# Second block's grouped attention: TensorE in the program's order, with half a gate tile between the parts of each step

## The chip, the cores and the metric

The kernel runs on one core of one Trainium2 chip. The metric is the time of one execution in microseconds (us), as the device measures it, and versions are compared by the median of several executions. The core's engines are named as in the profile: PE is TensorE's matmul side and PEld its weight loads, DVE is VectorE, ACT is ScalarE, POOL is GpSimd, and SP is SyncE, which here issues the loads from HBM.

## What is computed

The kernel computes two transformer blocks over 512 positions of width 1024. The change lies in the second block, between its recurrent branch (an mLSTM, `ym`) and the merge of two branches. Cut to what matters:

```python
scores = einsum(q, k)                    # 8 query heads on 2 key/value heads, 128-wide blocks
scores = where(valid, scores + bias, NEG_INF)
probs  = softmax(concat([scores, sink]))[..., :-1]
ya     = einsum(probs, v)                # grouped windowed attention
gates  = sigmoid(mg + merge_b)           # mg = h @ (merge columns of w_in), 2048 wide
u = gates[..., :1024] * (ya @ w_branch_attn) + gates[..., 1024:] * (ym @ w_branch_mlstm)
x = x + u @ w_out                        # then a mixture of 32 experts
```

The merge gates `mg` need only the normed input `h`. They depend neither on the attention `ya` nor on the recurrent branch `ym`.

## The kernel before

A scheduler at build time orders each engine's instructions by the program's order as a priority and by its own estimate of when their inputs are ready, so that work written later can stand between work written earlier. Inside `tc.manual_schedule(engines={PE})` it leaves PE's instructions in the order in which the program writes them, and still orders DVE, ACT and the others itself.

A dense product in this kernel is a tile of 128 outputs by 512 positions. `parts` splits the 512 KB of weights `wr` into a high part `wh` (ACT, L260) and a low part `wl` (DVE, L261), and `mm3` issues three matmuls for each of 8 slices of 128 inputs (L277 to L279), so a tile is 24 matmuls. The input is `hh` and `hl`, which the trace names `bh` and `bl` after their buffer; the sum lands in one of two PSUM buffers `d`. Small products use six PSUM buffers `m`.

At the place of the change the program writes, in this order:

- the end of the mLSTM. Per block of 128 positions POOL makes a norm (`rstd`), DVE applies it (L1247), and PE transposes the four heads (L1251). Then DVE (L1253, `nt`) and ACT and DVE (L260, L261, the trace's `hl<-nt`) make the split result `ym`, head by head.
- the attention, `_gqa`. Five groups of four transposes (L1290) bring queries and keys into place, ACT copies each group to `qk` (L1291). Then come 16 steps (t, i): four pairs of heads t, and four blocks of queries i. `scores(t, i)` multiplies queries and keys for the pair (PE, L1306, 256 keys wide at the first and last block and 384 in between), DVE adds the bias and takes the maximum (L1312), ACT exponentiates (L1317), DVE normalizes (L1318 to L1321) into `S`. `values(t, i)` transposes `S` (PE, L1333) and ACT copies it to `PT` (L1334); at i = 3 PE multiplies the whole pair's `PT` with the values (L1341) and the sum is split into `yah` and `yal`. `_pipelined` writes `scores` of a step and then `values` of the step before it.
- gate tiles 0 to 7: `mtanh(m)` computes a tile of `mg` and ACT takes its tanh (L700) into `tha`, which stays until the merge.
- the merge, `_merge`, which for each m computes gate tile 8 + m and then the two branch products.

Before the change nothing fixes PE's order here, and the scheduler puts matmuls of gate tiles 0 to 4 in the gaps of the mLSTM's end and of the attention.

Of the kernel before, what the change touches and what calls it, by code (L numbers as in the profile page):

```python
# [13 lines left out]
AF = mybir.ActivationFunctionType  # L14
# [3 lines left out]
P = 128  # L18
# [164 lines left out]
def _prog(ctx, tc, nc, I, out):  # L183
    PE, DVE, ACT, POOL, SP = nc.tensor, nc.vector, nc.scalar, nc.gpsimd, nc.sync
# [15 lines left out]
    def pt(pool, shape, tag, dt=F32, bufs=None):  # L200
        kw = {} if bufs is None else {"bufs": bufs}
        return pool.tile(shape, dt, tag=tag, name=nm(tag), **kw)
# [8 lines left out]
    def psd():  # L211
        return pt(pd, [P, 512], "d")
# [40 lines left out]
    def col(name, j=0, n=1):  # L253
        o, _ = _COLS[name]
        if kept:
            return kept[0][:, o - _COLS["final_norm_w"][0] + j :][:, :n]
        return cols[:, o + j : o + j + n]
# [5 lines left out]
    def raw(src, n=1024):  # L263
        r = ptx(W, [P, 1024], "wr")
        SP.dma_start(r[:, :n], src)
        return r[:, :n]

    def parts(r, pool=W):

        n = int(r.shape[1])  # L270
        hi, lo = (ptx(W, [P, 1024], n, F32R) if pool is W else pt(pool, [P, 1024], n, F32R, bufs=4) for n in ("wh", "wl"))
        split(hi[:, :n], lo[:, :n], r)
        return hi, lo

    def mm3(ps, w, x, first, last):
        (wh, wl), (xh, xl) = w, x
        PE.matmul(ps, lhsT=wh, rhs=xh, start=first, stop=False)  # L277
        PE.matmul(ps, lhsT=wl, rhs=xh, start=False, stop=False)  # L278
        PE.matmul(ps, lhsT=wh, rhs=xl, start=False, stop=last)  # L279

    def tile_a(src, x, kt=8, m=P):

        w = parts(raw(src, kt * m))
        ps = psd()
        for k in range(kt):
            mm3(ps[:m], [t[:, k * m : (k + 1) * m] for t in w], [t[:, k, :] for t in x], k == 0, k == kt - 1)
        ada_step()
        return ps
# [163 lines left out]
    def ada_step():  # L452
        if late[0]:
            late[0] -= 1
            late[1] += 1
            return
        next(ada_steps, None)
        if late[1]:
            late[1] -= 1
            next(ada_steps, None)  # L460
# [6 lines left out]
    with xps:  # L467

        hh = pt(HB, [P, 8, 512], "hh", F32R)
        hl = pt(HB, [P, 8, 512], "hl", F32R)  # L470
# [125 lines left out]
        hh = pt(HB, [P, 8, 512], "bh", F32R)  # L596
        hl = pt(HB, [P, 8, 512], "bl", F32R)
# [28 lines left out]
        with tc.tile_pool(name="ffn", bufs=2, reuse_waits="tile") as FF:  # L626
            x = (hh, hl)
            for part, (a, b) in enumerate(_PARTS):
                ah = pt(HB, [P, 8, 512], "hh", F32R)
                al = pt(HB, [P, 8, 512], "hl", F32R)  # L630
                for m in range(a, b):
                    y = []
                    for j in range(2):
                        ps = ups.pop(0) if ups else tile_a(I["w_up"][2 * m + j], x)
# [12 lines left out]
                for m in range(8 if part < 2 else 5):  # L647
                    ps = tile_a(dn(m), (ah, al), kt=b - a)
# [5 lines left out]
            hh = pt(HB, [P, 8, 512], "bh", F32R)  # L654
            hl = pt(HB, [P, 8, 512], "bl", F32R)
# [28 lines left out]
    with tc.tile_pool(name="b2", bufs=1, reuse_waits="tile") as B2:  # L684

        ym = pt(HB, [P, 8, 512], "hl", F32R)
        ymh, yml = ym[:, :4], ym[:, 4:]
        qkv = pt(B2, [P, 4, 768], "qkv")
        with tc.tile_pool(name="mq", bufs=1, reuse_waits="tile") as MQ:
            _mlstm(locals(), MQ)  # L690
        with tc.tile_pool(name="b2y", bufs=1, reuse_waits="tile") as B3:
            ya = pt(HB, [P, 8, 512], "hh", F32R)
            yah, yal = ya[:, :4], ya[:, 4:]
            mb = pt(B3, [P, 16], "mb")
            DVE.tensor_scalar(mb, col("merge_b", 0, 16), 0.5, None, op0=ALU.mult)

            def mtanh(m, pool):

                t = pt(pool, [P, 512], "tha%d" % m if m < 8 else "th", bufs=1 if m < 8 else 2)
                ACT.activation(t, tile_a(I["w2_mg"][m], (hh, hl)), AF.Tanh, bias=mb[:, m : m + 1], scale=0.5)  # L700
                return t

            _gqa(locals())
            tha = [mtanh(m, B3) for m in range(8)]
            xws.close()
            for n in places.values():
                n[1] = 0
            us = ExitStack()
            U = us.enter_context(tc.tile_pool(name="u", bufs=1, side="right", reuse_waits="tile"))
            uh = pt(U, [P, 8, 512], "uh", F32R)  # L710
            ul = pt(U, [P, 8, 512], "ul", F32R)
            _merge(locals())
# [558 lines left out]
def _gqa(env):  # L1271
    tc, nc, I, PE, DVE, ACT, POOL, SP = _names(env, "tc nc I PE DVE ACT POOL SP")
    pt, psd, psm, col, split = _names(env, "pt psd psm col split")
    yah, yal, qkv, sm, ident, pers = _names(env, "yah yal qkv sm ident pers")
    XW = env["XW"]
    rstd = env["rstd"]
    with tc.tile_pool(name="ga", bufs=1, reuse_waits="tile") as M:

        def bias_tile(h):
            b = pt(M, [P, 384], "bias", bufs=4)  # L1280
            SP.dma_start(b, I["t5b"][h])
            return b

        gq = pt(M, [P, 1], "gq")
        DVE.tensor_scalar(gq, col("q_gain"), 0.125, None, op0=ALU.mult)
        qk = pt(M, [P, 5, 512], "qk")
        for m in (4, 0, 1, 2, 3):
            ps = psm()
            for t in range(4):
                PE.transpose(ps[:, t * P : (t + 1) * P], qkv[:, t, m * P : (m + 1) * P], ident)  # L1290
            ACT.activation(qk[:, m, :], ps, AF.Copy, scale=gq if m < 4 else col("k_gain"))  # L1291
        state = {}

        def scores(t, i):
            if i == 0:
                state[t] = ([pt(M, [P, 10, P], "PT", bufs=3) for _ in range(2)], [bias_tile(2 * t), bias_tile(2 * t + 1)])
            _, bias = state[t]
            sink = col("sink", 2 * t, 2)
            J = range(max(0, i - 1), min(4, i + 2))
            n = len(J) * P  # L1300
            b0 = P if i == 0 else 0
            pss, Ss = [], []
            for e in range(2):
                ps = psm()
                r = slice(64 * e, 64 * e + 64)
                PE.matmul(ps[:, :n], lhsT=qk[r, t, i * P : (i + 1) * P], rhs=qk[r, 4, J[0] * P : J[0] * P + n], start=True, stop=True)  # L1306
                pss.append(ps)
            st = pt(sm, [P, 10], "st2", bufs=8)
            for e in range(2):
                S = pt(M, [P, 384], "S", bufs=6)  # L1310
                Ss.append(S)
                DVE.tensor_tensor_reduce(out=S[:, :n], in0=pss[e][:, :n], in1=bias[e][:, b0 : b0 + n], scale=1.0, scalar=sink[:, e : e + 1], op0=ALU.add, op1=ALU.max, accum_out=st[:, e : e + 1])  # L1312
            DVE.tensor_scalar(st[:, 2:4], st[:, 0:2], -1.0, None, op0=ALU.mult)
            DVE.tensor_tensor(st[:, 4:6], sink, st[:, 0:2], op=ALU.subtract)
            ACT.activation(st[:, 4:6], st[:, 4:6], AF.Exp)
            for e in range(2):
                ACT.activation(Ss[e][:, :n], Ss[e][:, :n], AF.Exp, bias=st[:, 2 + e : 3 + e], accum_out=st[:, 6 + e : 7 + e])  # L1317
            DVE.tensor_tensor(st[:, 4:6], st[:, 4:6], st[:, 6:8], op=ALU.add)  # L1318
            DVE.reciprocal(st[:, 8:10], st[:, 4:6])
            for e in range(2):  # L1320
                DVE.tensor_scalar(Ss[e][:, :n], Ss[e][:, :n], st[:, 8 + e : 9 + e], None, op0=ALU.mult)  # L1321
            return Ss

        bases = (0, 2, 5, 8)

        def values(t, i, Ss):
            PT, _ = state[t]
            J = range(max(0, i - 1), min(4, i + 2))
            n = len(J)
            for e in range(2):  # L1330
                tp = psm()
                for j in range(n):
                    PE.transpose(tp[:, j * P : (j + 1) * P], Ss[e][:, j * P : (j + 1) * P], ident)  # L1333
                ACT.activation(PT[e][:, bases[i] : bases[i] + n, :], tp[:, : n * P].rearrange("p (j q) -> p j q", j=n), AF.Copy)  # L1334
            if i == 3:
                po = psm()
                for i in range(4):
                    J = range(max(0, i - 1), min(4, i + 2))
                    for x, j in enumerate(J):
                        for e in range(2):  # L1340
                            PE.matmul(po[64 * e : 64 * e + 64, i * P : (i + 1) * P], lhsT=qkv[:, j, 640 + 64 * e : 704 + 64 * e], rhs=PT[e][:, bases[i] + x, :], start=(x == 0), stop=(x == len(J) - 1))  # L1341
                split(yah[:, t, :], yal[:, t, :], po)

        _pipelined([(t, i) for t in range(4) for i in range(4)], scores, values)


# [365 lines left out]
```

## Time and profile before

| what | value |
|---|---|
| three runs | 1588.38, 1591.37, 1591.61 us; median 1591.37 us |
| the profiled execution | 1588.89 us, of which 1587.1 us is the span between the first and the last instruction |
| busy PE, DVE, ACT in the span | 1550.4, 850.4, 524.4 us |
| granted TensorE clock, mean over the span | 0.992 of full speed |

The span is the stretch that the trace covers; what lies around it is 1.8 us. Times in the rows are counted from its start. Matmul records overlap, since one begins before the record of the one ahead has ended, so the pace of a run of matmuls is read from their starts and not from their durations.

### The profile page before, as it was taken

How to read it: one execution, taken by the hardware profiler on the slowest of the kernel's cores; microseconds unless marked ns; L12 is line 12 of the kernel's file. 1: busy time of each engine (PE TensorE's matmuls, PEld its weight loads, DVE VectorE, ACT ScalarE, POOL GpSimd, SP SyncE). 2: the span in 40 equal slices, each digit the busy share in tenths (PEclk: the TensorE clock that was granted, in tenths of full speed). 3: DMA queues.
4: the chain of work that ended last, by engine and by line, in shares of the span. 5: the costliest groups of instructions: out<-in, count | busy, mean ns of one | idle time of the engine just before them, and what ended most of it. 6: DMA issues, size and time to landing. Idle time of an engine off the chain costs nothing.

```text
span 1587.1 us, 21111 instructions
## 1 busy us (share of the span) xinstructions
PE 1550.4 (98%) x8208; PEld 1106.1 (70%) x8208; DVE 850.4 (54%) x1679; ACT 524.4 (33%) x964; POOL 35.8 (2%) x33
## 2 busy tenths in 40 slices
PE   8999999999999999989999999999999999999997
PEld 7878857988888888978976688866535545545443
DVE  7777886674564466668467724454242332332333
ACT  4453375442442344443456722231101101101101
POOL 0002000000000000000101000000000000000000
PEclk8999999999999999999999999999999999999999
DMA  8365423333233234402201023497999999999992
GB/s 331 135 197 175 167 73 101 126 100 106 100 94 104 95 93 128 145 18 98 89 27 57 29 86 98 141 316 271 392 369 418 418 415 418 419 417 417 418 417 75
DMA packets 92598, 321.02 MB, mean 202 GB/s; under 512 B 10412, under 2 KB 13100, under 8 KB 91472
## 3 DMA queue, kind: packets, MB, share of 16 engines
q1 hardware_dynamic: 92496, 319.64, 54.1%
q8 instruction: 66, 1.08, 0.3%
q14 instruction: 36, 0.29, 0.1%
HBM read 315.41 MB, written 4.19 MB: 201 GB/s over the span
## 4 chain that ended last, share of the span: by engine, by line
PE 90%; DVE 5%; ACT 2%; DMA 1%; issue 1%; POOL 1%; SPq 0%; DVEq 0%; ACTq 0%
PE d L1522 21%; PE d L277 15%; PE d L278 15%; PE d L279 15%; PE m L1508 4%; PE m L1624 4%; PE m L277 1%; PE m L279 1%; PE m L278 1%; PE m L1219 1%; PE m L1204 1%; DMA wr<-w_ada 1%; PE m L1039 1%; POOL rstd L371 1%; ACT S L1317 1%
## 5 line engine op out<-in xcount | busy, mean ns | idle before, releaser
L1522 PE MATMUL d<-we,xg 128*64 128x512 f32 x1024 | 226.6, 595 | 0.0
L261 DVE TENSOR_TENSOR wl<-wr,wh 128x1024 fp32r<-128x1024 f32 (+1 forms) x148 | 178.1, 1206 | 79.7 <-ACT wh L260 79.1
L277 PE MATMUL d<-bh,wh 128*128 128x512 f32 (+1 forms) x544 | 210.3, 387 | 2.6 <-ACT bh L475 1.5
L279 PE MATMUL d<-bl,wh 128*128 128x512 f32 (+1 forms) x544 | 209.7, 385 | 0.0
L278 PE MATMUL d<-bh,wl 128*128 128x512 f32 (+1 forms) x544 | 209.6, 385 | 0.0
L260 ACT ACTIVATE wh<-wr 128x1024 fp32r<-128x1024 f32 (+1 forms) x148 | 154.0, 1044 | 147.5 <-PE d L279 120.2
L1522 PEld LDWEIGHTS d<-we,xg 128*64 128x64 f32 x1024 | 70.8, 137 | 134.4 <-issue 121.6
L277 PE MATMUL d<-hh,wh 128*128 128x512 f32 (+1 forms) x392 | 147.2, 376 | 0.7 <-ACT bh L845 0.7
L278 PE MATMUL d<-hh,wl 128*128 128x512 f32 (+1 forms) x392 | 145.9, 373 | 0.0
L279 PE MATMUL d<-hl,wh 128*128 128x512 f32 (+1 forms) x392 | 145.8, 373 | 0.0
L277 PEld LDWEIGHTS d<-bh,wh 128*128 128x128 f32 x544 | 102.4, 188 | 25.0 <-issue 2.2
L278 PEld LDWEIGHTS d<-bh,wl 128*128 128x128 f32 x544 | 102.4, 188 | 22.2 <-issue 2.6
L279 PEld LDWEIGHTS d<-bl,wh 128*128 128x128 f32 x544 | 102.6, 189 | 20.1 <-issue 0.5
L1522 PE MATMUL d<-we,aT 128*64 128x512 f32 x512 | 112.6, 592 | 0.7 <-ACT aT L1597 0.7
L1522 PEld LDWEIGHTS d<-we,aT 128*64 128x64 f32 x512 | 36.7, 137 | 73.5 <-issue 71.4
L1625 DVE TENSOR_TENSOR xt<-xt,m 128x512 f32<-128x512 f32 x120 | 73.8, 681 | 22.8 <-PE m L1624 22.8
L277 PEld LDWEIGHTS d<-hh,wh 128*128 128x128 f32 x392 | 73.8, 188 | 16.8 <-issue 2.3
L1608 ACT ACTIVATE yh<-d,ws 128x512 fp32r<-128x512 f32 x32 | 22.0, 688 | 185.2 <-PE d L1522 185.2
L279 PEld LDWEIGHTS d<-hl,wh 128*128 128x128 f32 x392 | 73.7, 188 | 13.7 <-issue 0.5
L278 PEld LDWEIGHTS d<-hh,wl 128*128 128x128 f32 x392 | 73.9, 188 | 12.5
L638 DVE SCALAR_TENSOR_TENSOR cv<-d,cols,cv 128x511 f32<-128x511 f32 x41 | 30.7, 749 | 77.3 <-ACT cv L637 77.3
L1597 ACT ACTIVATE aT<-m 128x512 f32<-128x512 f32 x16 | 9.6, 598 | 176.5 <-PE m L1595 176.5
(430 smaller groups left out, 2631.6 us busy)
## 6 DMA issues: line engine op xcount, KB each, us to landing
we<-w_eg SPq DMA_DIRECT2D x128, 512.0 KB, 9.9
we<-w_eu SPq DMA_DIRECT2D x128, 512.0 KB, 8.9
we<-w_ed SPq DMA_DIRECT2D x128, 512.0 KB, 9.9
wr<-w_up SPq DMA_DIRECT2D x44, 512.0 KB, 3.3
wr<-w_ada SPq DMA_DIRECT2D x32, 512.0 KB, 4.0
wr<-w_out SPq DMA_DIRECT2D x16, 512.0 KB, 3.5
wr<-w_dn SPq DMA_DIRECT2D x16, 512.0 KB, 3.6
wr<-w_mg SPq DMA_DIRECT2D x16, 512.0 KB, 3.3
```

Source lines behind the costliest of these rows:

```text
L260: ACT.activation(hi, src, AF.Copy)
L261: DVE.tensor_tensor(lo, src, hi.bitcast(F32), op=ALU.subtract)
L277: PE.matmul(ps, lhsT=wh, rhs=xh, start=first, stop=False)
L278: PE.matmul(ps, lhsT=wl, rhs=xh, start=False, stop=False)
L279: PE.matmul(ps, lhsT=wh, rhs=xl, start=False, stop=last)
L371: POOL.tensor_tensor(r, ms, mhalf.to_broadcast((P, n)), op=ALU.pow)
L638: DVE.scalar_tensor_tensor(o[:, 1:], ps[:, :511], wc(1), o[:, 1:], op0=ALU.mult, op1=ALU.add)
L1508: PE.matmul(ps[:, :n], lhsT=hx[:, T, d * P : (d + 1) * P], rhs=oh[:, T, :n], start=(T == 0 and hx is hth), stop=(T == 3 and hx is htl))
L1522: PE.matmul(ps[x * m : (x + 1) * m], lhsT=xs[x][:, k, :], rhs=w[k // 2][x][:, k % 2 * 512 : k % 2 * 512 + 512], start=(k == 0), stop=(k == ...
L1608: ACT.activation(yh[:, s], ps, AF.Copy, scale=ws)
L1624: PE.matmul(ps, lhsT=oht[:, T * P : (T + 1) * P], rhs=y[:, s], start=(i == 0), stop=(i == len(mm) - 1))
L1625: DVE.tensor_tensor(xt[:, T, s], xt[:, T, s] if len(done) > 1 else hth[:, T, s].bitcast(F32), ps, op=ALU.add)
```

## The change

`mtanh` can now take a finished PSUM tile. A generator `mtanhs` computes gate tiles 0 to 7 and gives control back after four and after eight of the eight slices of each tile, so it has 16 pieces of 12 matmuls. `scores` takes the next piece at its end, and PE is in the program's order inside `_gqa`. The tiles are no longer written behind the attention.

```diff
-            def mtanh(m, pool):
+            def mtanh(m, pool, ps=None):
 
                 t = pt(pool, [P, 512], "tha%d" % m if m < 8 else "th", bufs=1 if m < 8 else 2)
-                ACT.activation(t, tile_a(I["w2_mg"][m], (hh, hl)), AF.Tanh, bias=mb[:, m : m + 1], scale=0.5)
+                ACT.activation(t, tile_a(I["w2_mg"][m], (hh, hl)) if ps is None else ps, AF.Tanh, bias=mb[:, m : m + 1], scale=0.5)
                 return t
 
+            tha = []
+
+            def mtanhs():
+
+                for m in range(8):
+                    w = parts(raw(I["w2_mg"][m]))
+                    ps = psd()
+                    for k in range(8):
+                        mm3(ps, [t[:, k * P : (k + 1) * P] for t in w], (hh[:, k, :], hl[:, k, :]), k == 0, k == 7)
+                        if k == 3:
+                            yield
+                    tha.append(mtanh(m, B3, ps))
+                    yield
+
+            fill = mtanhs()
             _gqa(locals())
-            tha = [mtanh(m, B3) for m in range(8)]
...
-    with tc.tile_pool(name="ga", bufs=1, reuse_waits="tile") as M:
+    fill = env["fill"]
+    with tc.tile_pool(name="ga", bufs=1, reuse_waits="tile") as M, tc.manual_schedule(engines={mybir.EngineType.PE}):
...
                 DVE.tensor_scalar(Ss[e][:, :n], Ss[e][:, :n], st[:, 8 + e : 9 + e], None, op0=ALU.mult)
+            next(fill)
             return Ss
```

The number of PE, DVE, ACT and DMA instructions stays the same. Three places show what moved. Lines of the changed file are 14 to 16 higher than those of the old one.

First, PE at the seam between the mLSTM's end and the first scores. In the old order gate tile 0 (`d_7901`) stands between the last transposes of the mLSTM (L1251) and those of queries and keys (L1290):

```order
L277 MATMUL d_7901<-bh_5206,wh_7897 128x512
L1251 MATMUL m_7264<-k_ident_92,hh_6665 128x128
L1251 MATMUL m_7273<-k_ident_92,hh_6665 128x128
L1251 MATMUL m_7282<-k_ident_92,hh_6665 128x128
L1251 MATMUL m_7291<-k_ident_92,hh_6665 128x128
L278 MATMUL d_7901<-bh_5206,wl_7898 128x512
L279 MATMUL d_7901<-bl_5207,wh_7897 128x512
L277 MATMUL d_7901<-bh_5206,wh_7897 128x512
L1290 MATMUL m_7327<-k_ident_92,qkv_5783 128x128 x4
L278 MATMUL d_7901<-bh_5206,wl_7898 128x512
L1290 MATMUL m_7333<-k_ident_92,qkv_5783 128x128 x4
```

In the new order the same transposes (L1265, L1305) follow one another, and gate tile 0 (`d_7377`) begins behind the first scores (L1321):

```order
L1265 MATMUL m_7264<-k_ident_92,hh_6665 128x128
L1265 MATMUL m_7273<-k_ident_92,hh_6665 128x128
L1265 MATMUL m_7282<-k_ident_92,hh_6665 128x128
L1265 MATMUL m_7291<-k_ident_92,hh_6665 128x128
L1305 MATMUL m_7329<-k_ident_92,qkv_5783 128x128 x4
L1305 MATMUL m_7335<-k_ident_92,qkv_5783 128x128 x4
L1305 MATMUL m_7341<-k_ident_92,qkv_5783 128x128 x4
L1321 MATMUL m_7353<-qk_7316 128x256
L1321 MATMUL m_7355<-qk_7316 128x256
L277 MATMUL d_7377<-bh_5206,wh_7373 128x512
```

All 39 gate matmuls that the old order has ahead of its first scores (24 of tile 0 and 15 of tile 1) moved behind them.

Second, PE in the attention's loop. In the old order the transposes of `S` (L1333) and the scores (L1306) of two steps stand together, and pieces of gate tiles of 7 to 11 matmuls stand at eight places, 73 matmuls in all, before the last product with the values:

```order
L279 MATMUL d_7934<-bl_5207,wh_7930 128x512
L277 MATMUL d_7934<-bh_5206,wh_7930 128x512
L1333 MATMUL m_7387<-k_ident_92,S_7356 128x128 x2
L1333 MATMUL m_7391<-k_ident_92,S_7358 128x128 x2
L1306 MATMUL m_7395<-qk_7314 128x384
L1306 MATMUL m_7397<-qk_7314 128x384
L1333 MATMUL m_7413<-k_ident_92,S_7374 128x128 x3
L1333 MATMUL m_7418<-k_ident_92,S_7376 128x128 x3
L1306 MATMUL m_7423<-qk_7314 128x256
L1306 MATMUL m_7425<-qk_7314 128x256
L278 MATMUL d_7934<-bh_5206,wl_7931 128x512
```

In the new order each step's transposes (L1349) and the next scores (L1321) are followed by 12 gate matmuls, 16 times:

```order
L278 MATMUL d_7454<-bh_5206,wl_7451 128x512
L279 MATMUL d_7454<-bl_5207,wh_7450 128x512
L1349 MATMUL m_7467<-k_ident_92,S_7395 128x128 x3
L1349 MATMUL m_7472<-k_ident_92,S_7397 128x128 x3
L1321 MATMUL m_7477<-qk_7316 128x256
L1321 MATMUL m_7479<-qk_7316 128x256
L277 MATMUL d_7454<-bh_5206,wh_7450 128x512
L278 MATMUL d_7454<-bh_5206,wl_7451 128x512
```

All 192 matmuls of gate tiles 0 to 7 now stand inside the loop, and none behind it.

Third, ACT at the same seam. In the old order gate tile 0's tanh (L700) and the high part of a later gate tile's weights (`wh_7996`) stand ahead of the last head's split and of the copies to `qk` (L1291):

```order
L260 ACTIVATE hl_5782<-nt_7287 128x512
L700 ACTIVATE tha_7894<-d_7901,mb_7307 128x512
L260 ACTIVATE wh_7996<-wr_7994 128x1024
L260 ACTIVATE hl_5782<-nt_7296 128x512
L1291 ACTIVATE qk_7314<-m_7315,cols_76 128x512
L1291 ACTIVATE qk_7314<-m_7321,gq_7312 128x512
```

In the new order these two are not there:

```order
L260 ACTIVATE hl_5782<-nt_7287 128x512
L260 ACTIVATE hl_5782<-nt_7296 128x512
L1306 ACTIVATE qk_7316<-m_7317,cols_76 128x512
L1306 ACTIVATE qk_7316<-m_7323,gq_7314 128x512
L1306 ACTIVATE qk_7316<-m_7329,gq_7314 128x512
```

They moved into the loop, where tanh and split now alternate with the steps. On DVE the matching low part (`wl_7997`) moved likewise. In SP's queue the eight gate loads stay ahead of the bias loads, and the load for gate tile 8 now stands ahead of the last bias pair, no longer behind all of them. POOL's order is unchanged.

## Rows read from the trace of the kernel before

**Rows 1.** The page, part 1: busy us, share of span, instructions.

```profile
PE 1550.4 (98%) x8208; PEld 1106.1 (70%) x8208; DVE 850.4 (54%) x1679; ACT 524.4 (33%) x964; POOL 35.8 (2%) x33
```

**Rows 2.** Stretches: length, busy (instructions) of PE, PEld, DVE, ACT, POOL, clock, DMA.

```profile
843.30:860.18 16.88, 14.11 (x76) 10.48 (x75) 12.78 (x23) 7.38 (x12) 4.91 (x4) 1.00 0.23 78
860.18:914.64 54.46, 51.63 (x379) 35.39 (x378) 40.38 (x166) 39.42 (x124) 0.00 (x0) 1.00 0.11 35
932.70:1079.00 146.30, 145.91 (x639) 113.71 (x637) 67.44 (x84) 43.38 (x55) 0.00 (x0) 1.00 0.52 178
1092.00:1566.00 474.00, 473.01 (x2402) 227.27 (x2403) 157.22 (x327) 57.70 (x95) 0.00 (x0) 1.00 0.96 388
```

**Rows 3.** PE's timeline around the first scores: start, duration, instruction, [idle before, releaser].

```profile
843.32 0.39 PE L277 MATMUL d<-bh,wh 128*128 128x512 f32 x1
...
845.97 0.63 PE L1251 MATMUL m<-k_ident,hh 128*128 128x128 f32 x4 [0.90 <-DVE hh L1247]
...
852.73 0.66 PE L1251 MATMUL m<-k_ident,hh 128*128 128x128 f32 x4 [1.01 <-DVE hh L1247]
...
859.86 0.39 PE L279 MATMUL d<-bl,wh 128*128 128x512 f32 x1
860.18 1.35 PE L1306 MATMUL m<-qk 64*128 64x256 f32 x8
...
864.18 0.63 PE L1333 MATMUL m<-k_ident,S 128*128 128x128 f32 x4 [0.85 <-DVE S L1321]
```

**Rows 4.** Timeline of ACT and DVE ahead of the first scores.

```profile
856.67 0.67 ACT L700 ACTIVATE tha<-d,mb 128x512 f32<-128x512 f32 x1
856.80 0.75 DVE L1253 SCALAR_TENSOR_TENSOR nt<-m,gh,hh 128x512 f32<-128x512 f32 x1
...
857.24 1.05 ACT L260 ACTIVATE wh<-wr 128x1024 fp32r<-128x1024 f32 x1
...
858.19 0.62 ACT L260 ACTIVATE hl<-nt 128x512 fp32r<-128x512 f32 x1
...
858.32 1.23 DVE L261 TENSOR_TENSOR wl<-wr,wh 128x1024 fp32r<-128x1024 f32 x1
...
859.28 1.26 ACT L1291 ACTIVATE qk<-m,gq 128x512 f32<-128x512 f32 x2
```

**Rows 5.** ACT's timeline: tanh behind two gate tiles that follow one another.

```profile
922.23 0.69 ACT L700 ACTIVATE tha<-d,mb 128x512 f32<-128x512 f32 x1 [3.80 <-PE d L279]
927.67 0.69 ACT L700 ACTIVATE tha<-d,mb 128x512 f32<-128x512 f32 x1 [4.75 <-PE d L279]
```

**Rows 6.** PE's timeline in the attention's loop.

```profile
881.64 0.88 PE L1333 MATMUL m<-k_ident,S 128*128 128x128 f32 x6
882.45 0.70 PE L1306 MATMUL m<-qk 64*128 64x256 f32 x4
883.08 0.50 PE L277 MATMUL d<-bh,wh 128*128 128x512 f32 x1
883.42 0.39 PE L278 MATMUL d<-bh,wl 128*128 128x512 f32 x1
...
885.69 2.40 PE L1341 MATMUL m<-PT,qkv 128*64 128x128 f32 x40
888.02 0.92 PE L1306 MATMUL m<-qk 64*128 64x384 f32 x4
888.87 0.66 PE L1333 MATMUL m<-k_ident,S 128*128 128x128 f32 x4
889.46 0.97 PE L1306 MATMUL m<-qk 64*128 64x384 f32 x4
```

**Rows 7.** Stretches with little matmul work and behind it; columns as in group 2.

```profile
22.00:28.00 6.00, 6.00 (x19) 5.23 (x20) 5.79 (x13) 3.40 (x5) 0.00 (x0) 0.50 0.92 350
711.00:714.00 3.00, 0.28 (x3) 0.08 (x1) 2.97 (x4) 0.85 (x2) 0.00 (x0) 1.00 0.03 5
714.50:717.50 3.00, 3.00 (x16) 3.00 (x15) 2.91 (x4) 0.96 (x2) 0.00 (x0) 0.50 0.51 175
```

## Prediction

> **What bounds the kernel now.** I first read the page's busy shares: PE has 98% and the next engine 54% [rows 1]. So the kernel is as long as PE's queue, and an edit is worth what it adds to or takes from the time in which PE does nothing useful. Next I read the stretches around the change [rows 2]. From 843.30, where the mLSTM's last dense tile has gone through PE, to the first scores at 860.18, PE is busy 14.11 of 16.88 us. In the attention's loop, up to the last product with the values, it is busy 51.63 of 54.46. Behind the gate tiles it is busy 145.91 of 146.30 us, and in the experts 473.01 of 474.00. So whatever the stretches up to the gates gain or lose reaches the end: the stretches behind have 0.39 + 0.99 = 1.4 us of waits that could take something up.
>
> The timeline then tells what PE is busy with ahead of the first scores [rows 3]. The reader should see two kinds of work. The transposes wait for DVE (0.90 and 1.01 us in the rows shown), because the mLSTM's end is a chain through POOL, DVE and ACT. Between them run gate matmuls, from 843.32 to 859.86, 39 of them by the order. They keep PE at work while the chain runs, and the chain doesn't need them. The first scores wait for the chain and not for PE: they start behind ACT's copies to `qk` [rows 4].
>
> **The change, step by step.** PE's work is the same in both orders, so I add up only differences of waiting and of pace.
>
> *The gate matmuls ahead of the first scores.* The new order puts none there. The chain goes on without them, and PE stands still where they ran. Their price is their pace: two gate tiles that follow one another end 927.67 - 922.23 = 5.44 us apart [rows 5], so a matmul takes 5.44 / 24 = 0.227 us, and 39 take **8.8 us**, which have to be done behind the first scores. This is the largest term. It would vanish if the scheduler could still move them, but inside the manual block PE's order is what stands there.
>
> *The chain to the first scores gets shorter.* ACT's tanh of gate tile 0 and a weight split stand no more ahead of the last head's split. That split started at 858.19, and its input was ready when DVE ended at 856.80 + 0.75 = 857.55 [rows 4]. So it can start about 0.6 us earlier, and the copies and the first scores with it: **-0.6**. It can't be much more, since everything ahead of that DVE row stays in its order, and not less than nothing.
>
> *Waits inside the loop.* Old: 54.46 - 51.63 = 2.8 us are shown idle [rows 2], as at 864.18, where transposes wait 0.85 us for `S` [rows 3]. In the new order 12 gate matmuls stand behind every scores. Between the scores of a step and its transposes lie two such pieces (2 x 2.7), the transposes of the step before (0.6 to 0.8) and the next scores (0.6 to 0.85) [rows 6], 6.7 to 7.1 us. The first step of old needed 864.18 - 860.18 = 4.0 us from scores to transposes [rows 3], and one weight split that gets between on DVE adds 1.23 [rows 4]: 5.2, still less. So these waits go, except at the last step, where only one piece, 2.7, six transposes, 0.8, and the scores themselves, 0.63, stand between, 4.2 in all against up to 5.2: a wait of about 0.8. Net **-2.0**. Bounds: nothing is saved if waits come back elsewhere. At the other end I price the loop from blocks that ran without a wait [rows 6]: per four steps one product with the values (888.02 - 885.69 = 2.33), two scores of 256 (0.63 each) and two of 384 (0.85), two groups of four transposes (0.59) and two of six (0.81), 8.1 us, four times 32.4; 73 gate matmuls, 16.6; eight entries into gate matmuls at 0.11 (883.42 - 883.08 = 0.34 against 0.227), 0.9. That makes 49.9, so up to 54.5 - 49.9 = 4.6 us could be waits that records partly cover. I take the idle that is shown, less the last step.
>
> *More entries.* 16 pieces instead of 8 cost 8 x 0.11 = **+0.9**.
>
> *The clock.* Between 843.3 and 859.6 PE now has only transposes. Where PE did 0.28 us of work in 3.0 us, the granted clock was at its lower level behind it, 0.50 (1.2 GHz), for at least 3.0 us of full work [rows 7]; near the start of the program it stayed there for 6.0 us. In half a clock's time half the work is lost: 1.5 to 3.0 us. I take **+2.0**, nearer to the single gap, with nothing as the lower bound, since the old stretch with its shorter waits kept 1.00 [rows 2].
>
> The Trainium skill, TensorE: Matmul & The Clock Gate, Part 4: PE-mode transpose, says that transposes don't count as TensorE work for the clock in the way that other matmuls do. By that rule the seam would count as a gap from end to end, and the sum would be the one below; if transposes did count, it would be 2 us less. No row here shows a stretch of transposes alone.
>
> *Edits at nothing.* The splits and tanhs that moved into the loop run on DVE and ACT, which were busy 40.38 and 39.42 of 54.46 us there [rows 2]; and the loop gets about 27 us longer with the 119 matmuls (27.0 us) that move into it, so they are covered. Should one be late, PE would wait up to its 1.23 us. The load of gate tile 8 ahead of the last bias pair in SP's queue has the length of the loop as cover; without it the first merge tile would wait.
>
> Sum: 8.8 - 0.6 - 2.0 + 0.9 + 2.0 = **+9.1 us**. The profiled execution took 1588.89 us (span 1587.1 and 1.8 around it), so it would become 1598.0. It lies 2.5 below the median of the three runs, and 1.2 below the mean of all four times (1590.06). I add the 1.2 and forecast **1599**.
>
> **The rivals.**
>
> *The clock stays up.* Then the term of 2.0 is missing and the time is 1597. For it speaks that the old seam, with 2.8 us of waits, kept 1.00 [rows 2]; against it that of the new seam's 16.3 us only 14.11 - 8.8 = 5.3 hold matmuls.
>
> *No difference.* The delay is taken up: all 4.6 us of the loop's possible waits go, the clock stays up, and later waits absorb their 1.4. That leaves 8.8 - 0.6 - 4.6 + 0.9 - 1.4 = 3.1, a time of about 1593. Against it: PE's idle behind the gates is made of small waits on other engines that move along with PE.
>
> *Faster.* One mechanism: in the loop the old order loses far more than the shown idle to handing over between engines, and the regular pieces win it back. To be 3.2 us faster, the loop would have to give back 8.8 - 0.6 + 0.9 + 3.2 = 12.3 us, 0.77 for each of 16 steps; the time would be 1587 or less. The blocks allow 4.6 [rows 6], so little speaks for it.
>
> *Much slower.* The steps become bound by the chain on DVE and ACT: if scores to transposes took 8.1 us instead of at most 5.2, because a step's small operations queue behind splits, each of 16 steps would wait about 1 us, and the time would be about 1615. It decides from 6.7 us on. Against it stands the 4.0 of the first step.
>
> **How the numbers follow.** What a measurement of this kernel can tell from no change is about 0.2%, 3.2 us. Forecast with the lower clock: 0.74. Clock up: 0.10. No difference: 0.08. Faster: 0.03. Much slower: 0.05. Slower holds the first, second and last, 0.89; same 0.08; faster 0.03. The range: least, 8.8 - 0.6 - 4.6 + 0.9 = +4.5 on the fastest time, 1588.4, gives 1593; most, 8.8 + 0.9 + 3.0 and nothing gained is +12.7 on the slowest, 1591.6, gives 1604. It leaves out the rivals faster and much slower and part of no difference, under 2 in 10.
>
> **What the profile after would show.** Right: between the mLSTM's last dense tile and the first scores PE shows waits on DVE and ACT of about 11 us, with no L277 to L279; the first scores start at about 859.6; the granted clock there or just behind it is at 0.50; in the loop PE waits 1 us or less, most of it ahead of the last L1349; the first tile of the merge starts about 9 us later than before, and everything behind keeps its length. Wrong: gate matmuls ahead of the first scores; first scores far ahead of 859; waits of L1349 at every step; or a merge and experts that get shorter by what the seam loses.

## The result: 0.55% slower, and the profile after

The changed kernel took 1598.38 us (median of five runs, 1596.49 to 1601.93), the kernel before 1590.81 beside it (1588.38 to 1591.61): a ratio of 1.0055, with a 95% interval of 1.0038 to 1.0073. A second set gave 1.0041 (1.0028 to 1.0055; the run `e10_changed_again`, below). The profiled execution took 1596.49 us, with a span of 1594.7.

The two spans differ by 7.6 us. Two instructions that stand on either side of the change tell how much of it is the change's: the last matmul of the mLSTM's last dense product (its weights are called om, so the last om matmul below), and ACT's tanh of gate tile 8, the first gate tile of the merge. In the timeline of PE and of ACT before they are these:

```profile
843.09 0.39 PE L279 MATMUL d<-bl,wh 128*128 128x512 f32 x1
938.55 0.69 ACT L700 ACTIVATE th<-d,mb 128x512 f32<-128x512 f32 x1 [3.80 <-PE d L279]
```

That is 95.46 us from start to start. In the changed kernel PE's timeline around the first scores, which answers to [rows 3], with the tanh of ACT's timeline as its last line, reads:

```profile
845.98 0.39 PE L279 MATMUL d<-bl,wh 128*128 128x512 f32 x1
848.86 0.63 PE L1265 MATMUL m<-k_ident,hh 128*128 128x128 f32 x4 [2.49 <-DVE hh L1261]
...
853.72 1.12 PE L1265 MATMUL m<-k_ident,hh 128*128 128x128 f32 x4 [1.59 <-DVE hh L1261]
855.62 1.11 PE L1265 MATMUL m<-k_ident,hh 128*128 128x128 f32 x4 [0.78 <-DVE hh L1261]
...
862.45 0.70 PE L1321 MATMUL m<-qk 64*128 64x256 f32 x4 [2.15 <-ACT qk L1306]
863.08 0.50 PE L277 MATMUL d<-bh,wh 128*128 128x512 f32 x1
863.42 0.40 PE L278 MATMUL d<-bh,wl 128*128 128x512 f32 x1
...
947.64 0.69 ACT L700 ACTIVATE th<-d,mb 128x512 f32<-128x512 f32 x1 [5.10 <-PE d L279]
```

The stretch is now 947.64 - 845.98 = 101.66 us, **6.20 longer**. The seam, from that matmul to the first scores, went from 860.18 - 843.09 = 17.09 to 16.47; the loop, from the first scores to the tanh, from 78.37 to 85.19. No gate matmul is left in the seam, and PE waits there for DVE and ACT. The rest of the 7.6 lies outside: the changed kernel reaches the seam 2.9 us later and is 1.5 us quicker in the routing (last section).

The stretches answer to [rows 2], with the same columns:

```profile
846.20:862.45 16.25, 8.61 (x38) 6.23 (x37) 11.63 (x22) 5.79 (x10) 4.90 (x4) 0.68 0.24 81
862.45:941.90 79.45, 79.08 (x497) 59.04 (x497) 45.01 (x170) 46.54 (x133) 0.00 (x0) 0.98 0.10 33
943.30:1088.00 144.70, 144.22 (x631) 112.33 (x630) 67.33 (x91) 41.74 (x53) 0.00 (x0) 1.00 0.53 184
1100.00:1574.00 474.00, 473.32 (x2404) 227.41 (x2404) 157.24 (x327) 57.64 (x95) 0.00 (x0) 1.00 0.96 389
```

In the seam PE is busy 8.61 of 16.25 us, and at a clock of 0.68. In the loop it is shown idle for 0.37 us, where it was 2.8. Behind the gates nothing changed.

The clock by stretches, with the same columns (to [rows 7]):

```profile
850.50:860.00 9.50, 6.65 (x28) 4.94 (x26) 6.67 (x12) 1.89 (x3) 2.92 (x2) 0.50 0.42 139
860.20:863.60 3.40, 1.25 (x7) 0.78 (x7) 2.15 (x7) 2.99 (x6) 0.00 (x0) 0.99 0.00 0
863.90:866.90 3.00, 3.00 (x8) 2.32 (x8) 1.35 (x8) 1.41 (x6) 0.00 (x0) 0.50 0.01 3
867.30:872.00 4.70, 4.70 (x24) 3.11 (x24) 1.92 (x9) 1.87 (x6) 0.00 (x0) 1.00 0.00 0
```

It fell to 0.50 (1.2 GHz) while PE had only transposes and waits, came back in a stretch in which PE did 1.25 us of work in 3.4, and fell again in the middle of the first gate piece. Eight matmuls took 3.0 us there; behind it 24 records fit into 4.7.

The end of the loop in PE's timeline (to [rows 6]):

```profile
929.75 0.92 PE L1321 MATMUL m<-qk 64*128 64x384 f32 x4
...
933.47 0.82 PE L1349 MATMUL m<-k_ident,S 128*128 128x128 f32 x6
934.22 0.70 PE L1321 MATMUL m<-qk 64*128 64x256 f32 x4
...
937.48 0.39 PE L279 MATMUL d<-bl,wh 128*128 128x512 f32 x1
937.71 0.82 PE L1349 MATMUL m<-k_ident,S 128*128 128x128 f32 x6
938.89 0.67 PE L1349 MATMUL m<-k_ident,S 128*128 128x128 f32 x4 [0.37 <-DVE S L1336]
939.50 2.40 PE L1357 MATMUL m<-PT,qkv 128*64 128x128 f32 x40
```

The last step is the only one whose transposes are shown to wait, 0.37 us. It has one piece as cover; its scores began 938.89 - 934.22 = 4.67 us earlier.

### The profile page after: what moved, and what is told of

The parts are those of the page before. It is cut to its first block, busy times and chain, and to the rows that moved or that the text cites. A ratio compares the mean times of both kernels' runs of the same rounds, so it can differ in the third digit from the quotient of the medians.

```text
span 1594.7 us, 21106 instructions
## 1 busy us (share of the span) xinstructions
PE 1556.1 (98%) x8208; PEld 1111.9 (70%) x8208; DVE 850.4 (53%) x1679; ACT 524.1 (33%) x964; POOL 35.8 (2%) x33
## 4 chain that ended last, share of the span: by engine, by line
PE 90%; DVE 4%; DMA 2%; ACT 1%; issue 1%; POOL 1%; SPq 0%; DVEq 0%; ACTq 0%
PE d L1538 21%; PE d L277 16%; PE d L279 15%; PE d L278 15%; PE m L1524 4%; PE m L1640 4%; PE m L277 1%; PE m L278 1%; PE m L279 1%; PE m L1233 1%; PE m L1218 1%; PE m L1053 1%; POOL rstd L371 1%; PE m L1321 1%; PE m L1016 1%
```

## The experiments

Theory: the loss sits in the seam (gate matmuls missing there, and the clock behind it), while the regular pieces in the loop win back more waits than the profile showed. Rivals: the loop wins back only the 2.0 us of the prediction; the clock costs nothing; the pieces themselves cost time. Times of a run are medians, and the ratio is to the kernel before on the same chip; the stretch is that from the last om matmul to the tanh of gate tile 8, from one profile of each, and seam and loop are its two parts. In e2, e7 and e8 the seam holds 48, 96 and 144 gate matmuls, so there only the whole stretch compares.

| run | time, us | ratio (95%) | seam | loop | stretch |
|---|---|---|---|---|---|
| before | 1590.8 | | 17.09 | 78.37 | 95.46 |
| after | 1598.4 | 1.0055 (1.0038 to 1.0073) | 16.47 | 85.19 | 101.66 |
| e10, after again | 1596.9 | 1.0041 (1.0028 to 1.0055) | 16.32 | 85.29 | 101.61 |
| e1, pieces, order free | 1588.9 | 0.9991 (0.9982 to 1.0000) | 17.08 | 75.89 | 92.97 |
| e2, two tiles ahead | 1586.4 | 0.9978 (0.9969 to 0.9987) | 19.11 | 72.82 | 91.93 |
| e3, seam alone | 1599.4 | 1.0060 (1.0045 to 1.0075) | 16.47 | 88.40 | 104.87 |
| e4, dummies | 1602.9 | 1.0086 (1.0070 to 1.0101) | 23.28 | 83.60 | 106.88 |
| e5, fewer dummies | 1597.4 | 1.0041 (1.0027 to 1.0055) | 18.42 | 83.59 | 102.01 |
| e6, products | 1596.7 | 1.0042 (1.0028 to 1.0055) | 16.47 | 83.58 | 100.05 |
| e7, pieces of 6 | 1590.2 | 1.0002 (0.9992 to 1.0011) | 29.99 | 65.02 | 95.01 |
| e8, pieces of 3 | 1592.4 | 1.0012 (1.0003 to 1.0022) | 40.87 | 57.22 | 98.09 |
| e9, transposes twice | 1596.4 | 1.0044 (1.0028 to 1.0059) | 16.42 | 83.60 | 100.02 |
| e11, twice again | 1597.6 (one run) | | 16.43 | 83.63 | 100.06 |

**e1_free**: the generator, without the manual block.

```diff
-    with tc.tile_pool(name="ga", ...) as M, tc.manual_schedule(engines={mybir.EngineType.PE}):
+    with tc.tile_pool(name="ga", ...) as M:
```

> The gates stay in pieces of 12 at the ends of scores, but PE isn't held to the program's order. By the build's order 39 gate matmuls then stand ahead of the first scores again, and the pieces of 12 between the steps stay from the seventh step on. I read the stretch from the last om matmul ahead of the seam to the tanh of gate tile 8: 95.46 us before, 101.66 after. Theory (the loss sits in the seam, and the pieces in the loop win back 4.5 us of waits): 95.46 - 4.5 + 0.9 = 91.9 us, time about 1587. Rival (the loop can only win the 2.0 us that the prediction took, the rest of the stage's difference is something else): 94.4 us, time about 1590. If the pieces themselves cost time: 96 us or more.

The seam is that of before again (17.08), and the stretch 92.97 us lies between the two theories. This order still waits in the loop; the view of PE's waits says by whom, for whom, us in total, times, and the longest:

```profile
PE m L1349 <- DVE S L1336: 1.4, 3, 0.9
```

Its time is only just below that of before, though the stretch is 2.5 us shorter. In the profiled execution DVE waited for a reload of `x` late in the kernel, and PE for DVE 1.6 us (before 0.3); whether the other executions lose time there too, no profile shows. The first line is DVE's, the second PE's:

```profile
DVE x L777 <- DMA x<-x2d: 9.2, 5, 4.5
PE m L785 <- DVE x L778: 1.6, 1, 1.6
```

**e2_two_tiles_ahead**: two gate tiles written behind the transposes of queries and keys, the rest in 16 pieces of 9 (48 slices), the manual block around the loop alone.

```diff
+        for _ in range(6):
+            next(fill)
         state = {}
...
-                        if k == 3:
+                        if k == 7:
+                            tha.append(mtanh(m, B3, ps))
+                        if (8 * m + k) % 3 == 0:
                             yield
-                    tha.append(mtanh(m, B3, ps))
-                    yield
...
-        _pipelined([(t, i) for t in range(4) for i in range(4)], scores, values)
+        with tc.manual_schedule(engines={mybir.EngineType.PE}):
+            _pipelined([(t, i) for t in range(4) for i in range(4)], scores, values)
```

> Gate tiles 0 and 1 are written ahead of the attention's loop and free to go into the seam, PE is in the program's order in the loop alone, and each of the 16 steps takes 9 gate matmuls instead of 12. Theory (seam covered, loop waits gone as long as two pieces, 2 x 2.0, with 1.4 to 1.6 of transposes and scores, 5.5 in all, are longer than the chain of at most 5.2 us): stretch from the last om matmul to the tanh of gate tile 8 is 91.9 us, time about 1587. Rival (pieces of 9 are too short to cover the chain): waits of L1349-like transposes at most steps, 95 us or more, time 1590 or more.

91.93 us, as the theory has it, and **faster than both kernels**: the interval lies wholly below 1. The build puts 48 gate matmuls ahead of the first scores, between the same transposes as in [rows 3]. Written so, PE's order comes out the same without the manual block: it is the place of the pieces that counts. PE's waits in the loop are those of the last step alone:

```profile
PE m L1351 <- DVE S L1338: 0.4, 1, 0.4
```

With as many entries into gate matmuls as after (0.9 by the prediction's term), the loop wins back 95.46 - 91.93 + 0.9 = 4.4 us. What is measured is the net, 3.5; the 4.4 rests on that term. The rival's 2.0 would have given 94.4, so it is out.

**e3_seam_alone**: the first gate matmuls are held behind the first scores, the rest is free and behind the attention.

```diff
+        first = ExitStack()
+        first.enter_context(tc.manual_schedule(engines={mybir.EngineType.PE}))
...
-            next(fill)
+            if (t, i) == (0, 0):
+                next(fill)
+                first.close()
...
             _gqa(locals())
+            list(fill)
...
-                        if k == 3:
+                        if m == 0 and k == 0:
```

> Only the first half of the change: the first gate matmul is held behind the first scores, and the rest of the loop is left to the build's order, as before the change. Stretch from the last om matmul to the tanh of gate tile 8: with 4.5 us of waits that the regular pieces win back it is 101.66 + 4.5 - 0.9 = 105.3 us; if they win back 2.0, as the prediction took, 102.8 us. PE in the seam as after: no gate matmuls, granted clock at 0.50 there.

104.87 us, near the theory. But some of it is the clock's, which stayed low for longer: the first 10 us from the first scores are at 0.75 here and at 0.83 after.

```profile
858.44:868.44 10.00, 9.85 (x38) 5.38 (x39) 5.90 (x27) 5.97 (x18) 0.00 (x0) 0.75 0.00 1
```

```profile
862.45:872.45 10.00, 10.00 (x40) 6.88 (x40) 4.44 (x20) 5.18 (x16) 0.00 (x0) 0.83 0.00 1
```

Without these 0.8 us the loop's pieces win back 104.87 - 0.8 - 101.66 + 0.9 = 3.3 us, halfway between the theories, and its loop isn't that of before step for step. So alone it doesn't decide; it does show that the first half of the change costs all that is lost and more.

**e4_dummy_in_seam**: `dummy(n)` multiplies the identity by itself n times, ahead of the mLSTM's heads 0, 2 and 3, and ahead of the first scores. `ip` keeps these products and the mLSTM's transposes in the program's order, head by head, so the edit also moves the transposes of queries and keys behind them.

```diff
+    def dummy(n, ip=lambda i: i):
+        if n:
+            ps = psm()
+        for _ in range(n):
+            ip(PE.matmul(ps[:, :P], lhsT=ident, rhs=ident, start=True, stop=True))
...
             for h in range(4):
+                env['dummy']((14, 0, 14, 6)[h], ip)
...
-                    PE.transpose(ps[:, T * P : (T + 1) * P], hS[:, T, h * P : (h + 1) * P], ident)
+                    ip(PE.transpose(ps[:, T * P : (T + 1) * P], hS[:, T, h * P : (h + 1) * P], ident))
...
+        env["dummy"](14)
         state = {}
```

> The changed kernel with 48 products of the identity with itself (thrown away) in the seam's waits, 14, 14, 6 and 14 of them. Theory (the slow clock behind the seam costs 1.6 us): granted clock 1.00 behind the first scores, first gate piece at 0.23 us a matmul instead of 0.43, stretch from the last om matmul to the tanh of gate tile 8 at 101.66 - 1.6 = 100.1 us. Rival (the clock falls all the same, or what looks like its loss is covered): 101.7 us. If the dummies get in the chain's way the first scores start later than 16.5 us behind the last om matmul, and the stretch is 101.7 or more.

Both halves came. The loop took 83.60 us, 1.6 less than after, with the clock up behind the first scores. But each product is two records of 0.12 us, twice what I had assumed, and the scores started 6.8 us later. Inside the seam the clock fell all the same, behind a wait of 3.65 us (columns as above):

```profile
851.20:857.90 6.70, 5.28 (x24) 4.99 (x25) 3.49 (x5) 1.26 (x2) 1.01 (x1) 0.50 0.49 173
```

**e5_fewer_dummies**: 8, 6, 2 and 6 of them.

> As the run with 14, 14, 6 and 14 identity products, but 8, 6, 2 and 6, since each took twice the time assumed and they stood in the chain's way (first scores 6.8 us later). Theory (the slow clock behind the seam costs 1.6 us, and nothing else changes): first scores about 16.5 us behind the last om matmul, granted clock at 1.00 in the first gate piece, stretch from the last om matmul to the tanh of gate tile 8 at 100.1 us. Rival (so few dummies don't hold the clock): granted clock 0.50 behind the first scores and 101.7 us.

The clock term again (loop 83.59; in the seam the clock fell here too), and again the scores came later, by 2.0 us. In both runs dummies stand right ahead of the transposes of heads 2 and 3, which the chain needs, so a filler must not stand ahead of work that the chain is waiting for. How much of the delay is the transposes' new order, no run separates.

**e6_seam_products**: the seam's transposes as products.

```diff
-                    PE.transpose(ps[:, T * P : (T + 1) * P], hS[:, T, h * P : (h + 1) * P], ident)
+                    PE.matmul(ps[:, T * P : (T + 1) * P], lhsT=hS[:, T, h * P : (h + 1) * P], rhs=ident, start=True, stop=True)
...
-                PE.transpose(ps[:, t * P : (t + 1) * P], qkv[:, t, m * P : (m + 1) * P], ident)
+                PE.matmul(ps[:, t * P : (t + 1) * P], lhsT=qkv[:, t, m * P : (m + 1) * P], rhs=ident, start=True, stop=True)
```

> The changed kernel with the seam's 36 transposes (of the normed heads, and of queries and keys) written as plain products with the identity, which give the same values. If what is missing for the clock is that kind of work, the granted clock is 1.00 behind the first scores and the stretch from the last om matmul to the tanh of gate tile 8 is 100.1 us. If it is the waiting (7 us of the 16.5), the clock is 0.50 all the same and the stretch 101.7 us, or more where a product takes longer than a transpose. The Trainium skill, TensorE: Matmul & The Clock Gate, Part 4: PE-mode transpose, by which transposes count less than other matmuls, speaks for the first.

100.05 us: the seam as long as after, at a granted clock of 1.00, and the loop 85.19 - 83.58 = **1.61 us** shorter. That is the clock's price, shown by itself in the stretch; the ratios of the times, 1.0042 here and 1.0041 in e10, are too coarse for it. The stretches from the last om matmul to the first scores, and 10 us behind them:

```profile
843.07:859.54 16.47, 9.97 (x75) 8.49 (x73) 11.83 (x22) 5.80 (x10) 4.90 (x4) 1.00 0.25 80
859.54:869.54 10.00, 10.00 (x46) 6.86 (x47) 5.76 (x25) 6.45 (x17) 0.00 (x0) 1.00 0.01 2
```

It doesn't tell the kind of work from its amount, since a product is twice the records of a transpose.

**e9_transposes_twice** and **e11_twice_again**: transposes, each done twice into the same place.

```diff
-                    PE.transpose(ps[:, T * P : (T + 1) * P], hS[:, T, h * P : (h + 1) * P], ident)
+                    [PE.transpose(ps[:, T * P : (T + 1) * P], hS[:, T, h * P : (h + 1) * P], ident) for _ in range(2)]
...
-                PE.transpose(ps[:, t * P : (t + 1) * P], qkv[:, t, m * P : (m + 1) * P], ident)
+                [PE.transpose(ps[:, t * P : (t + 1) * P], qkv[:, t, m * P : (m + 1) * P], ident) for _ in range(2)]
```

> With products in place of transposes the clock stayed up and the stretch fell to 100.05 us, but a product with the identity also keeps PE busy about twice as long as a transpose (four take 1.16 us against 0.6). Here each of the seam's 36 transposes is done twice, so PE is as busy as with the products, with transposes alone. If the amount of work decides: granted clock 1.00 in the first gate piece, stretch from the last om matmul to the tanh of gate tile 8 at 100.1 us. If the kind of work decides (transposes don't hold the clock, as the earlier expectation cites): clock 0.50 behind the first scores and 101.7 us, more if the doubled transposes at the slow clock reach the chain.

> The run with each of the seam's transposes done twice, once more and unedited, since its profile (granted clock 1.00 from the last om matmul on) is a single one and speaks against the rule that the prediction cited. If the doubled transposes hold the clock: granted clock 1.00 in the seam and behind it, stretch from the last om matmul to the tanh of gate tile 8 at 100.0 us again. If it was chance: clock 0.50 behind the first scores, 101.6 us.

100.02 and 100.06 us. The seam of e9 has transposes alone, and the clock stays up:

```profile
844.97:861.39 16.42, 9.51 (x74) 7.76 (x72) 11.83 (x22) 5.79 (x10) 4.90 (x4) 1.00 0.24 80
861.39:871.39 10.00, 9.99 (x46) 6.84 (x47) 5.74 (x25) 6.47 (x17) 0.00 (x0) 1.00 0.01 2
```

So transposes alone can hold the clock, and it was the amount of work and not its kind that decided, as far as two profiles at 1.00 beside three with single transposes at 0.50 (after, e10, e3) can tell. The amount over the whole seam isn't enough, though: e4 and e5 have PE busy for 18.07 and 12.06 us there, and their clock fell at a wait of 3.65 us. The 1.6 us are too few to be seen in the times of these runs beside those of e10.

**e7_pieces_of_6** and **e8_pieces_of_3**: as e2, with four and six tiles ahead and 2 slices or 1 to a piece. These are the lines of e7 against e2; e8 has 48 and every slice in their place.

```diff
-        for _ in range(6):
+        for _ in range(16):
...
-                        if (8 * m + k) % 3 == 0:
+                        if (8 * m + k) % 2 == 1:
```

> As with two tiles ahead of the loop, but four tiles ahead and 6 gate matmuls in each step. Work is the same as with pieces of 9, so the stretch from the last om matmul to the tanh of gate tile 8 would be 91.9 us but for waits. Between the scores of a step and its transposes then lie two pieces (2 x 1.36), six transposes (0.8) and twice the scores (0.85), 5.2 us. In the changed kernel the same chain took 4.67 us at the last step and 6.0 where a weight split (1.2 us) lay in it. Theory (waits start where the cover is shorter than the chain): 0.8 us at the steps with a split, some 2 to 3 us in all, 94 to 95 us. Rival (the chain is as long at every step, 6.0): 0.8 at 12 steps, 101 us. Rival (the chain shortens when there are fewer splits): 92 us.

> Six tiles ahead of the loop and 3 gate matmuls in each step: the cover is 2 x 0.68 + 0.8 + 1.7 = 3.9 us. Theory: waits of 0.8 us or more at the 12 steps that have no product with the values, stretch from the last om matmul to the tanh of gate tile 8 at 102 us or more, slower than before (95.46). Rival (cover hardly matters, the loop of before lost its time elsewhere): 92 to 95 us.

95.01 and 98.09 us, where pieces of 9 gave 91.93: the cover matters, with less for each step than I expected of pieces of 3. PE's waits in the loop, of e7 and of e8:

```profile
PE m L1351 <- DVE S L1338: 1.3, 4, 0.3
```

```profile
PE m L1351 <- DVE S L1338: 4.9, 7, 1.2
```

The chain of e8 is a little shorter than that of the changed kernel: its first transposes start 890.23 - 885.77 = 4.46 us behind their scores of 256 keys, where the last step of the changed kernel took 4.67. That fewer weight splits in the loop are the reason is likely, not shown. The timeline also shows what the view of waits leaves out:

```profile
885.77 0.70 PE L1323 MATMUL m<-qk 64*128 64x256 f32 x4
...
888.71 0.40 PE L279 MATMUL d<-bl,wh 128*128 128x512 f32 x1
890.23 0.67 PE L1351 MATMUL m<-k_ident,S 128*128 128x128 f32 x4 [1.13 <-DVE S L1338]
```

The transposes start 1.52 us behind the last gate matmul, where a matmul's pace is 0.23: 1.29 us are lost, and 1.13 shown. A record is longer than the pace, so each wait is shown some 0.16 us short, and waits of up to 0.3 us aren't marked at all. Over e7's loop 95.01 - 91.93 = 3.1 us are lost against e2, and 1.3 shown.

**e10_changed_again**: the changed kernel, unedited.

> The changed kernel once more, unedited, beside the kernel before, for the size of the difference. By the stretch around the change the traces differ by 6.2 us, and all the rest between them (2.9 us longer ahead of it, 1.5 us shorter in the routing) lies in work that is the same in both. If that rest is chance, the ratio comes out near 1.004 (1596.5 us); if it belongs to the change, at 1.0055 again (1599).

1.0041, so the rest of 7.6 - 6.2 = 1.4 us between the two spans looks like chance, though the two intervals overlap. The stretch repeated to 0.05 us.

## Why the prediction was right, and where its sum was off

The direction, the mechanism and the range held. The sum, +9.1 us, was too large by 2.9 against the stretch's +6.2 (6.5 by the second set, 1596.92 - 1590.44); that the first median, 1598.38, came out next to 1599 owes something to chance.

- **Gate matmuls ahead of the first scores, 8.8.** Right: none stands there now, and PE waited instead. e2 gives them back: 101.66 - 91.93 = 9.7 us, against 8.8 + 1.6 of clock - 0.6 of chain = 9.8.
- **The chain, -0.6.** Right: 17.09 - 16.47 = 0.62. ACT's last split starts at 860.61, behind DVE's `nt` that ends at 859.83 + 0.75 = 860.58 (before 0.64 later, [rows 4]):

```profile
859.83 0.75 DVE L1267 SCALAR_TENSOR_TENSOR nt<-m,gh,hh 128x512 f32<-128x512 f32 x1
```

```profile
860.61 0.63 ACT L260 ACTIVATE hl<-nt 128x512 fp32r<-128x512 f32 x1 [0.82 <-DVE nt L1267]
861.15 0.67 ACT L1306 ACTIVATE qk<-m,cols 128x512 f32<-128x512 f32 x1
```

- **Waits in the loop, -2.0: the step that failed in size.** "I take the idle that is shown, less the last step" was the wrong one of the two bounds. Priced from blocks as the prediction did, the loop of before, up to the tanh of gate tile 8, is 177 gate matmuls (40.2), 32.4 for the steps and 9 entries (1.0); of 78.37 us 4.8 are waits. With the clock up (e6) the new loop is 216 gate matmuls (49.0), 32.4 and 17 entries (1.9); of 83.58 us 0.3 are waits. So **4.5** came back, and e2 says 4.4; both take 0.11 for an entry. The shown 2.8 was short because each wait is shown short (e8's timeline). The starts say it without a price: the step from the last gate matmul of a piece to the transposes behind it takes 0.23 us at all 15 places in the changed kernel's loop (937.48 to 937.71), and 0.48 to 1.23 at the eight places of before, 3.9 us more than eight times 0.23 in all. One of them, which isn't marked as a wait:

```profile
869.24 0.39 PE L277 MATMUL d<-bh,wh 128*128 128x512 f32 x1
869.73 0.94 PE L1333 MATMUL m<-k_ident,S 128*128 128x128 f32 x6
```

- **Entries, +0.9.** The first gate matmul of a piece starts 0.34 us ahead of the second (863.08, 863.42), as in [rows 6], and the account above closes with it. No run took it alone.
- **The clock, +2.0.** It measured 1.6 (85.19 against 83.58 to 83.63 in five profiles with the clock up). The row came as foreseen, 0.50 in the seam and once more behind it. The rule that I cited beside it, from the Trainium skill, TensorE: Matmul & The Clock Gate, Part 4: PE-mode transpose, that transposes don't count for the clock as other matmuls do, isn't what these traces show: transposes done twice held it at 1.00 in two of two profiles, and so did products. Of the signs, the waits in the seam came out at 16.25 - 8.61 = 7.6 us and not about 11: at the lower clock four transposes take up to 1.12 us instead of 0.63.
- **Behind the gates, nothing.** From the tanh of gate tile 8 to the copy of the router's logits 142.45 us before and 142.54 after.

Of the rivals, **no difference** had its first part right, the loop's 4.5, but not the clock, and nothing later took up the delay. **Much slower** did not come, since the cover was long enough: the scores of 384 at 929.75 had their transposes at 937.71, 8.0 us later, and their `S` was ready at 934.98 + 0.75 = 935.73, after 6.0. The prediction had 7.1 and 5.2 at most: it left the step's own scores out of the cover, and the chain was longer than it allowed. That the two errors cancel is luck.

```profile
934.98 0.75 DVE L1336 TENSOR_SCALAR S<-S,st 128x384 f32<-128x384 f32 x2
```

**Faster** failed for the change as it was, but its mechanism is e2's: the loop gives back its 4.5 if the seam keeps its gate matmuls.

## What to carry to other kernels

Work that depends on nothing should first fill the longest wait near it, and only what is left should be spread evenly over a loop; the change did the second by taking from the first. A piece is long enough when two of them, with what else lies between a result's making and its use, outlast the chain on the other engines: 9 matmuls were, 6 and 3 weren't. Take lost time from starts and a priced account, since idle as shown hides short waits.

## What was not expected

Two stretches that the change doesn't touch vary between executions more than some of its terms. The last om matmul starts anywhere from 841.97 to 847.36 us in the 13 profiles. Between before and after 2.9 us of this arise, most of it near the start. The granted clock differs there, and so does the DMA's share; which of them makes the difference isn't shown. PE's busy time, clock and DMA, before and then after:

```profile
12.00:32.00 20.00, 17.83 (x89) 0.74 0.98 392
```

```profile
12.00:32.00 20.00, 17.37 (x72) 0.66 0.90 342
```

And the routing, from the copy of the router's logits to the first gather matmul, takes 11.2 to 11.3 us in seven profiles and 9.8 in the other six. Between them lies the pace of the 28 records of dummy products with zeros on PE: 8.00 us before, at a clock of 0.84 over the stretch, and 6.31 after, at 1.00.

```profile
1081.60:1092.30 10.70, 10.07 (x48) 8.69 (x48) 7.58 (x41) 0.74 (x3) 0.00 (x0) 0.84 0.98 347
```

```profile
1090.80:1100.00 9.20, 8.58 (x49) 7.47 (x49) 7.62 (x41) 0.74 (x3) 0.00 (x0) 1.00 0.99 349
```

So a difference of 1 to 3 us between two single times of this kernel says little, while the length of one stretch between two named instructions repeated to 0.05 us.
